# A retention block's group norm: v's rows freed of their mean ahead of the split, the variance from ScalarE's squares, the gate product as a plain instruction

## The chip, the cores and the metric

The kernel runs on one core of a Trainium2 chip. The core has TensorE (PE, matrix products into eight banks of PSUM), VectorE (DVE), ScalarE (ACT), GpSimd (POOL, which also issues DMAs) and SyncE (SP, which issues DMAs). Each engine works through its own queue in order and waits for others by semaphores. The metric is device time in microseconds (us), less is better. The kernel before takes 1023.57 us, the median of three runs from 1023.52 to 1023.67.

## The reference

One layer of a bidirectional encoder on x of 512 tokens by 1024 features, in float32: a combined projection of the normed x, a gated short convolution, a bidirectional retention with four heads, a merge of both with two gates, a SwiGLU feed-forward part and a last norm. What the change touches is the retention's end. With P[n, m] the decayed scores of a head (512 by 512, both directions together) and v its values (512 tokens by 512 features):

```
ret = P @ v                                   # per head, 512 x 512
mu  = mean(ret, over the 512 features)
var = mean((ret - mu)^2, over the 512 features)
ret = (ret - mu) * rsqrt(var + EPS) * g_ret
y_r = (ret * silu(g_sw)) @ w_r_out
```

The mean of a row of ret is the same sum over m, with P's weights, of the means of v's rows. If every row of v has mean zero, mu is zero for every row of ret, and var is the mean of its squares.

## The kernel before

Every float32 product is done as three products of a high and a low part (`mm3`, lines 340 to 344): a factor is rounded into its high part by ScalarE and the rest is taken by VectorE, in `split` (lines 200 to 210). Weights come by DMA into raw tiles, are split the same way (lines 203 and 204) and used from five buffers.

The work runs in this order: projections (to about 378 us), the retention heads (378 to 602 us), the output projections with a Strassen scheme, the feed-forward part, the last norm. q, k, v and the swish gate sg of each head were written to DRAM earlier and are loaded again one head ahead by `load_head` (lines 858 to 861), at the top of the iteration before.

The loop of the heads (lines 948 to 967) does, for head h:

- `do_pv(p, vv, sg)` (lines 884 to 905): for each of four blocks of 128 rows, twelve products into one bank (128 x 512), ret of these rows. VectorE reads the bank for the statistics (`bn_stats`, line 894; `bn_aggr`, 895), adds EPS (896); POOL raises to the power of -1/2 (897); VectorE forms (ret - mu) times the gate from the bank (903), which sets the bank free; ScalarE scales the result by the power (905). Behind the last block's power POOL issues four DMAs that add up weights for W_o in DRAM (`sum_step`, lines 265 to 274, of which 272 adds and 274 copies).
- `do_scores` for head h + 1 (lines 863 to 876): four banks of 24 products in all, times the decay table on VectorE (873), split into p.
- `split_v` for head h + 1 (lines 878 to 882): two calls of `split` on halves of 128 x 1024.
- `do_t` for head h (lines 907 to 913): sixteen transposes on VectorE (line 218), then four scaled splits (206 on ScalarE, 207 on VectorE) into yr.
- the convolution's last part (`do_mix(3)`, for h = 0), or `do_wr(h - 1)` (lines 927 to 940): the product of the head before with its rows of W_r, two halves of four banks with 48 products each; the banks are emptied by ScalarE (935, for head 0) or VectorE (937).

The convolution's `z_forms` (lines 789 to 806) of `do_mix` runs beside the first blocks of `do_pv` of heads 0 and 1; it uses up to ten scratch tiles of 128 x 512 (`t512`, nine buffers) that are free again when POOL's DMAs (line 633) have stored them.

Nothing in this code fixes the order on an engine but the `issue_after` blocks. A scheduler orders the instructions of each engine when the program is built: by its model of the times, among those that are ready the one that comes first in the program. Buffers of a pool are handed out in that order too. So an edit at one place can shift the order elsewhere.

Of the kernel before, what the change touches and what calls it, by code (L numbers as in the profile page):

```python
# [12 lines left out]
F32 = mybir.dt.float32  # L13
F32R = mybir.dt.float32r
AF = mybir.ActivationFunctionType
ALU = mybir.AluOpType

P = 128
# [3 lines left out]
NB = S // P  # L22
HEADS = 4
QK = 256
VD = 512
FF = 2816
NFB = FF // P
EPS = 1e-6
# [143 lines left out]
def block_kernel(ctx: ExitStack, tc: tile.TileContext, xw0, xw, xT, xtok, wpack, wquad, cols, decs, rot, g_ffn, g_final, out):  # L172
    nc = tc.nc
# [5 lines left out]
    small = ctx.enter_context(tc.tile_pool(name="small", bufs=4))  # L179
# [8 lines left out]
    def bigtile(dt=F32, n=4):  # L188
        return big.tile([P, n, 512], dt, tag="big", name="big", padded_shape=[P, 4, 512])

    def t512(dt=F32):
        return tmp.tile([P, 512], dt, tag="t512", name="t512")

    def bank():
        return psum.tile([P, 512], F32, tag="bank", name="bank")
# [4 lines left out]
    def split(src, hi, lo, scale=None, round=None):  # L200

        if scale is None:
            first = (round or nc.scalar.copy)(hi, src)  # L203
            low_of[0] = nc.vector.tensor_tensor(out=lo, in0=src, in1=hi.bitcast(F32), op=ALU.subtract)  # L204
        else:
            first = nc.scalar.activation(hi, src, AF.Copy, scale=scale)
            nc.vector.scalar_tensor_tensor(
                out=lo, in0=src, scalar=scale, in1=hi.bitcast(F32),
                op0=ALU.mult, op1=ALU.subtract)
        return first  # L210
# [54 lines left out]
    def sum_step(behind, among="quads"):  # L265

        if steps[among]:
            quad, f, g, u, add = steps[among].pop(0)
            src = wsum[quad, g, u] if g[0] == "t" else quarter(quad, g, u)
            with tc.issue_after(behind.ins):  # L270
                if add:
                    nc.gpsimd.dma_start(out=wsum[quad, f, u], in_=src, accum_op=ALU.add, max_dma_last_dim=4 * CH)
                else:
                    nc.gpsimd.dma_start(wsum[quad, f, u], src)
# [65 lines left out]
    def mm3(ps, left, right, first, last):  # L340
        (lh, ll), (rh, rl) = left, right
        nc.tensor.matmul(ps, lh, rh, start=first, stop=False)  # L342
        nc.tensor.matmul(ps, lh, rl, start=False, stop=False)  # L343
        nc.tensor.matmul(ps, ll, rh, start=False, stop=last)  # L344
# [293 lines left out]
    for h in range(EARLY):  # L638
        pss = [bank() for _ in range(4)]
        for kk in range(8):  # L640
# [4 lines left out]
            if (h, kk) == (1, 1):  # L645
# [3 lines left out]
                for k in range(8):  # L649
                    xk = x_in(k)  # L650
                    nc.vector.scalar_tensor_tensor(out=xs[k // 4][:, k % 4, :], in0=xk, scalar=gmix[:, k:k + 1], in1=rrow,
                                                   op0=ALU.mult, op1=ALU.mult)
# [13 lines left out]
        t = bigtile()  # L666
# [21 lines left out]
    for n, i, o in (("a11", 0, 0), ("a12", 1, 0), ("a22", 1, 256)):  # L688
# [16 lines left out]
                            op0=ALU.mult, op1=ALU.add)  # L705
    for j in range(15, 0, -2):
# [3 lines left out]
                                   op0=ALU.mult, op1=ALU.mult)  # L710
# [166 lines left out]

    def split_v(v):
        vv = (bigtile(F32R), bigtile(F32R))
        for k in (0, 2):  # L880
            split(v[:, k:k + 2, :], vv[0][:, k:k + 2, :], vv[1][:, k:k + 2, :])
        return vv

    def do_pv(p, vv, sg):

        for nb in range(NB):
            ps = bank()
            sl = slice(nb * P, (nb + 1) * P)
            for mb in range(NB):
                mm3(ps, (p[0][:, mb, sl], p[1][:, mb, sl]), (vv[0][:, mb, :], vv[1][:, mb, :]),  # L890
                    mb == 0, mb == NB - 1)
            st = small.tile([P, 6], F32, tag="bnst", name="bnst")
            mv = small.tile([P, 4], F32, tag="bnmv", name="bnmv")
            nc.vector.bn_stats(st, ps)
            nc.vector.bn_aggr(mv[:, 0:2], st)
            nc.vector.tensor_scalar_add(mv[:, 2:3], mv[:, 1:2], EPS)
            power = nc.gpsimd.tensor_tensor(out=mv[:, 3:4], in0=mv[:, 2:3], in1=mhalf[:, 0:1], op=ALU.pow)
            if nb == NB - 1:

                for _ in range(4):  # L900
                    sum_step(power, "heads")
            t = sg[:, nb, :]
            nc.vector.scalar_tensor_tensor(out=t, in0=ps, scalar=mv[:, 0:1], in1=t,
                                           op0=ALU.subtract, op1=ALU.mult)
            nc.scalar.activation(t, t, AF.Copy, scale=mv[:, 3:4])

    def do_t(h, t):
# [35 lines left out]
    nxt = load_head(0)  # L943
    p = do_scores(nxt[0], nxt[1])
    vv, sg = split_v(nxt[2]), nxt[3]
    do_mix(2)
    yr = None
    for h in range(HEADS):
        if h < HEADS - 1:
            nxt = load_head(h + 1)  # L950
        else:
            load_z((0,))
        do_pv(p, vv, sg)
        t = sg
        if h < HEADS - 1:
            p = do_scores(nxt[0], nxt[1])
            vv, sg = split_v(nxt[2]), nxt[3]
        else:
            load_z((1, 2))
        new = do_t(h, t)  # L960
        if h == 0:
            do_mix(3)
        else:
            if h == HEADS - 1:
                sgr = [load(t) for t in grd]
            do_wr(h - 1, yr)
        yr = new
# [456 lines left out]
```

## Time and profile before

| | before |
|---|---|
| timed runs, median (lowest to highest) | 1023.57 us (1023.52 to 1023.67) |
| profiled execution: span, first to last instruction | 1021.7 us |
| TensorE clock granted, mean | 0.999 |
| busy: PE, weight load, DVE | 1013.2, 883.2, 902.5 us |
| busy: ACT, POOL | 548.4, 151.7 us |
| instructions | 14821 |
| DMA | 202.34 MB, mean 198 GB/s |

The profile is of one execution. Its own time is given as the span; the timed runs are measured from outside of it. Busy time counts an engine's instructions, not the waits and the issuing of DMAs. PEld is the load of weights into the array, which overlaps the products. In a row of grouped instructions stand line, engine, operation, output and inputs with partitions x elements, the count, then busy time in us and the mean of one in ns, then idle time of the engine just ahead of them and what ended it. In a timeline a row has its start and its length in us; several like instructions in a row are merged, with their count. A wait has the waiting instruction, what it waited for, the sum in us, how often, and the longest.

### The profile page before, as it was taken

Reading aid. Unit: us, or ns where it says so; the run is one execution under the profiler, and the core shown is the slowest. Engines: PE = TensorE matmul, PEld = TensorE weight load, DVE = VectorE, ACT = ScalarE, POOL = GpSimd, SP = SyncE. Lnnn points to the kernel's source line nnn. Section 1 sums busy time; section 2 is a strip of 40 time slices with the busy share of each in tenths; the row PEclk is TensorE's granted clock in tenths of the full one; section 3 lists DMA queues with packets and bytes.
Section 4 is the critical chain, followed back from the end, with each engine's and each line's share of the span. In section 5 each row is a group of like instructions: output and inputs, shape, how many; then the busy total and the mean of one; then the engine's idle time right before and its main releaser. Section 6 shows DMA issues by size and latency. Waiting matters only on the chain.

```text
span 1021.7 us, 14821 instructions
## 1 busy us (share of the span) xinstructions
PE 1013.2 (99%) x5586; PEld 883.2 (86%) x5586; DVE 902.5 (88%) x1161; ACT 548.4 (54%) x744; POOL 151.7 (15%) x238
## 2 busy tenths in 40 slices
PE   9999999999999999999999999999999999999997
PEld 7888888888888998888888888889998999899986
DVE  7878998979798888797989997999898999889996
ACT  7547665553655455343543325586654565556554
POOL 0030221222122003202122100020001410110011
PEclk9999999999999999999999999999999999999999
DMA  9525587695767657839597855484316562663523
GB/s 354 188 81 185 173 296 212 214 310 162 249 196 238 250 203 268 333 130 349 124 331 294 272 200 169 157 264 132 107 42 242 172 154 83 198 153 104 165 69 98
DMA packets 53992, 202.34 MB, mean 198 GB/s; under 512 B 7392, under 2 KB 7520, under 8 KB 49312
## 3 DMA queue, kind: packets, MB, share of 16 engines
q1 hardware_dynamic: 37600, 137.39, 39.0%
q0 software_dynamic: 16032, 63.71, 21.3%
q8 instruction: 44, 0.72, 0.3%
q10 hardware_dynamic: 288, 0.29, 0.1%
q14 instruction: 28, 0.23, 0.1%
HBM read 162.82 MB, written 57.41 MB: 216 GB/s over the span
## 4 chain that ended last, share of the span: by engine, by line
PE 98%; DVE 1%; ACT 0%; issue 0%; POOL 0%; POOLq 0%; ACTq 0%
PE bank L427 39%; PE bank L383 27%; PE bank L342 10%; PE bank L343 10%; PE bank L344 10%; PE bank L477 0%; PE bank L1053 0%; PE bank L998 0%; PE bank L662 0%; DVE raw L301 0%; DVE big L1296 0%; ACT whi L203 0%; DVE wlo L204 0%; POOL fin L1286 0%; POOL ac L1035 0%
## 5 line engine op out<-in xcount | busy, mean ns | idle before, releaser
L203 ACT CAST whi<-raw 128x1024 fp32r<-128x1024 f32 (+2 forms) x299 | 302.8, 1028 | 265.0 <-PE bank L427 67.1
L204 DVE TENSOR_TENSOR wlo<-raw,whi 128x1024 fp32r<-128x1024 f32 (+2 forms) x300 | 352.7, 1192 | 68.0 <-ACT whi L203 67.7
L383 PE MATMUL bank<-xform,whi 128*128 128x256 f32 x1424 | 258.2, 284 | 0.3 <-ACT whi L203 0.3
L383 PEld LDWEIGHTS bank<-xform,whi 128*128 128x128 f32 x1424 | 222.3, 192 | 2.0 <-ACT t L434 0.8
L383 PE MATMUL bank<-xform,wlo 128*128 128x256 f32 x712 | 200.7, 283 | 0.0
L427 PE MATMUL bank<-whi,big 128*128 128x512 f32 x596 | 187.0, 389 | 0.0
L427 PE MATMUL bank<-whi,xform 128*128 128x512 f32 x496 | 157.1, 390 | 0.0
L301 DVE TENSOR_TENSOR raw<-raw 128x1024 f32<-128x1024 f32 (+1 forms) x128 | 152.0, 1203 | 4.2 <-DMA raw<-wquad 3.3
L383 PEld LDWEIGHTS bank<-xform,wlo 128*128 128x128 f32 x712 | 136.4, 192 | 0.0
L427 PEld LDWEIGHTS bank<-whi,big 128*128 128x128 f32 x596 | 111.9, 188 | 23.8 <-ACT t L434 0.4
L427 PE MATMUL bank<-wlo,big 128*128 128x512 f32 x298 | 115.7, 389 | 0.0
L427 PEld LDWEIGHTS bank<-whi,xform 128*128 128x128 f32 x496 | 93.0, 188 | 19.7 <-DVE xform L204 0.6
L427 PE MATMUL bank<-wlo,xform 128*128 128x512 f32 x248 | 96.5, 389 | 0.0
L434 ACT COPY t<-bank 128x512 f32<-128x512 f32 x105 | 61.0, 587 | 56.3 <-PE bank L383 30.1
L342 PE MATMUL bank<-big,whi 128*128 128x512 f32 x220 | 85.7, 390 | 0.0
L344 PE MATMUL bank<-big,wlo 128*128 128x512 f32 x220 | 85.6, 389 | 0.0
L343 PE MATMUL bank<-big,whi 128*128 128x512 f32 x220 | 85.6, 389 | 0.0
L427 PEld LDWEIGHTS bank<-wlo,big 128*128 128x128 f32 x298 | 56.0, 188 | 11.4
L427 PEld LDWEIGHTS bank<-wlo,xform 128*128 128x128 f32 x248 | 46.6, 188 | 9.6
L342 PE MATMUL bank<-whi,big 128*128 128x512 f32 x128 | 49.8, 389 | 0.0
L343 PE MATMUL bank<-wlo,big 128*128 128x512 f32 x128 | 49.8, 389 | 0.0
L344 PE MATMUL bank<-whi,big 128*128 128x512 f32 x128 | 49.8, 389 | 0.0
(203 smaller groups left out, 1385.8 us busy)
## 6 DMA issues: line engine op xcount, KB each, us to landing
raw<-wquad SPq DMA_DIRECT2D x140, 512.0 KB, 4.7
raw<-wpack SPq DMA_DIRECT2D x42, 512.0 KB, 6.3
t_f<-wquad POOLq DMA_DIRECT2D x12, 512.0 KB, 8.0
z<-t POOLq DMA_DIRECT2D x24, 256.0 KB, 4.5
t_o<-wquad POOLq DMA_DIRECT2D x12, 512.0 KB, 6.7
zform<-z POOLq DMA_DIRECT2D x6, 1024.0 KB, 7.8
v<-t POOLq DMA_DIRECT2D x16, 256.0 KB, 5.7
sg<-t POOLq DMA_DIRECT2D x16, 256.0 KB, 4.8
```

The lines of the kernel that those rows point to most:

```text
L203: first = (round or nc.scalar.copy)(hi, src)
L204: low_of[0] = nc.vector.tensor_tensor(out=lo, in0=src, in1=hi.bitcast(F32), op=ALU.subtract)
L301: nc.vector.tensor_tensor(out=t, in0=t, in1=raws[quad, more, u][:, 0:n], op=ALU.add)
L342: nc.tensor.matmul(ps, lh, rh, start=first, stop=False)
L343: nc.tensor.matmul(ps, lh, rl, start=False, stop=False)
L344: nc.tensor.matmul(ps, ll, rh, start=False, stop=last)
L383: nc.tensor.matmul(o, l[:, c], r[:, k], start=start and s == 0 and k == 0 and i == 0, stop=stop and k == 3 and i == 2, skip_group_check=True)
L427: nc.tensor.matmul(pss[tt], l, r[:, c], start=start and k == 0 and i == 0, stop=stop and k == n - 1 and i == 2, skip_group_check=True)
L434: nc.scalar.copy(t, ps)
```

## The change

In `split_v` each row of v (a token, on its partition) gets the mean of its 512 features taken away ahead of the split. ScalarE copies each of four 128 x 512 parts onto itself with a running sum; POOL multiplies the four sums by -1/512; ScalarE writes the high part as a copy of v plus that number, and VectorE the low part as v plus the number less the high part. Two casts and two subtractions of 128 x 1024 become four sums, one small product, four shifted copies and four subtractions with a scalar operand of 128 x 512.

In `do_pv` the two instructions of the statistics go. ScalarE squares the bank, scaled by 1/sqrt(512), into a scratch tile that nobody reads, with a running sum, which is the variance. The addition of EPS moves from VectorE to POOL. The gate product no longer takes the mean away and is a product of two operands. A bank is now free when both ScalarE's squares and the gate product have read it.

```
@@ split_v
         vv = (bigtile(F32R), bigtile(F32R))
-        for k in (0, 2):
-            split(v[:, k:k + 2, :], vv[0][:, k:k + 2, :], vv[1][:, k:k + 2, :])
+        m = small.tile([P, 8], F32, tag="mean", name="mean")
+        for k in range(NB):
+            nc.scalar.activation(v[:, k, :], v[:, k, :], AF.Copy, accum_out=m[:, k:k + 1])
+        nc.gpsimd.tensor_scalar_mul(m[:, 4:8], m[:, 0:4], -1.0 / VD)
+        for k in range(NB):
+            off = m[:, 4 + k:5 + k]
+            nc.scalar.activation(vv[0][:, k, :], v[:, k, :], AF.Identity, bias=off)
+            nc.vector.scalar_tensor_tensor(out=vv[1][:, k, :], in0=v[:, k, :], scalar=off,
+                                           in1=vv[0][:, k, :].bitcast(F32), op0=ALU.add, op1=ALU.subtract)
         return vv
@@ do_pv
-            st = small.tile([P, 6], F32, tag="bnst", name="bnst")
             mv = small.tile([P, 4], F32, tag="bnmv", name="bnmv")
-            nc.vector.bn_stats(st, ps)
-            nc.vector.bn_aggr(mv[:, 0:2], st)
-            nc.vector.tensor_scalar_add(mv[:, 2:3], mv[:, 1:2], EPS)
+            nc.scalar.activation(t512(), ps, AF.Square, scale=VD ** -0.5, accum_out=mv[:, 1:2])
+            nc.gpsimd.tensor_scalar_add(mv[:, 2:3], mv[:, 1:2], EPS)
             power = nc.gpsimd.tensor_tensor(out=mv[:, 3:4], in0=mv[:, 2:3], in1=mhalf[:, 0:1], op=ALU.pow)
...
-            nc.vector.scalar_tensor_tensor(out=t, in0=ps, scalar=mv[:, 0:1], in1=t,
-                                           op0=ALU.subtract, op1=ALU.mult)
+            nc.vector.tensor_tensor(out=t, in0=ps, in1=t, op=ALU.mult)
             nc.scalar.activation(t, t, AF.Copy, scale=mv[:, 3:4])
```

## The prediction

> **What bounds the kernel now.** I read the page first (busy shares, chain), then the waits of TensorE (PE), then the busy time by stretches, then the timelines around the retention heads, where all edits lie.
>
> ```profile
> span 1021.7 us, 14821 instructions
> ...
> PE 1013.2 (99%) x5586; PEld 883.2 (86%) x5586; DVE 902.5 (88%) x1161; ACT 548.4 (54%) x744; POOL 151.7 (15%) x238
> ...
> PE 98%; DVE 1%; ACT 0%; issue 0%; POOL 0%; POOLq 0%; ACTq 0%
> ```
> ```profile
> PE bank L477 <- DVE t L474: 1.4, 1, 1.4
> PE bank L1053 <- DVE t L1039: 0.5, 1, 0.5
> PE bank L383 <- ACT whi L203: 0.3, 1, 0.3
> ```
> ```profile
> 378.50:602.30 223.80, 223.80 (x1011) 186.06 (x1010) 198.85 (x306) 86.16 (x119) 45.93 (x74) 1.00 0.75 258
> 602.30:690.00 87.70, 87.07 (x427) 72.82 (x427) 79.63 (x98) 56.07 (x81) 6.30 (x12) 1.00 0.61 198
> 690.00:800.00 110.00, 109.66 (x791) 103.19 (x790) 100.62 (x122) 65.58 (x90) 4.46 (x8) 1.00 0.43 139
> ...
> 1004.00:1021.70 17.70, 11.61 (x52) 9.28 (x50) 10.67 (x20) 7.69 (x20) 4.11 (x8) 0.96 0.32 119
> ```
> The first fence: PE is busy 1013.2 of 1021.7 us, and 98% of the chain that ended last is PE. The second is the whole list of what PE ever waited for: 1.4 us at the start, 0.5 and 0.3 us far behind the heads. The third (columns: stretch, length, then busy time of PE, weight load, VectorE (DVE), ScalarE (ACT), GpSimd (POOL), then clock, DMA) puts the heads into 378.5 to 602.3: PE is busy for every one of the 223.8 us, at clock 1.00. VectorE has 199 us of work in it, ScalarE 86. So the change works on engines that are nowhere last in their stage. What is idle on PE and could come back behind the heads is 0.63 us (87.70 less 87.07) and 0.34 us (110.00 less 109.66); the 6.1 us at the end are the tail of the last norm, which the change doesn't touch. No gain can be over 0.97 us unless PE itself gets less work, and it gets none: the edits leave every matmul.
>
> The span, 1021.7, is what the sum is made against. The timed runs have a median of 1023.57, which is 1.87 more; that lies outside the first and last instruction, and I carry it unchanged.
>
> **The change part by part.** The rows of the terms, from the grouped lines (count, busy us, mean ns of one, idle before):
>
> ```profile
> L937 DVE TENSOR_TENSOR big<-bank,big 128x512 f32<-128x512 f32 x24 | 15.3, 682 | 0.1
> L903 DVE SCALAR_TENSOR_TENSOR big<-bank,bnmv,big 128x512 f32<-128x512 f32 x16 | 11.9, 742 | 0.0
> L894 DVE BATCH_NORM_STATS2 bnst<-bank 128x6 f32<-128x512 f32 x16 | 11.1, 692 | 1.5 <-PE bank L344 1.5
> ...
> L204 DVE TENSOR_TENSOR big<-big 128x1024 fp32r<-128x1024 f32 x8 | 9.7, 1217 | 0.0
> ...
> L779 DVE SCALAR_TENSOR_TENSOR big<-u,cols_sb,big 128x512 f32<-128x512 f32 x8 | 6.0, 750 | 0.9 <-ACT big L777 0.8
> ...
> L895 DVE BATCH_NORM_AGGREGATE bnmv<-bnst 128x2 f32<-128x6 f32 x16 | 2.9, 180 | 1.1
> ...
> L896 DVE TENSOR_SCALAR bnmv<-bnmv 128x1 f32<-128x1 f32 x16 | 2.5, 153 | 0.5
> ```
> ```profile
> L905 ACT ACTIVATE big<-big,bnmv 128x512 f32<-128x512 f32 x16 | 11.4, 722 | 28.6 <-POOL bnmv L897 27.4 <-DVE big L903 1.3
> ...
> L203 ACT CAST big<-t 128x512 fp32r<-128x512 f32 x16 | 9.7, 616 | 5.9 <-DVE t L873 5.9
> L203 ACT CAST big<-big 128x1024 fp32r<-128x1024 f32 x8 | 8.4, 1049 | 0.0
> ...
> L935 ACT COPY big<-bank 128x512 f32<-128x512 f32 x8 | 4.1, 603 | 0.0
> ```
> ```profile
> L1031 ACT ACTIVATE t<-big 128x512 f32<-128x512 f32 x8 | 5.0, 629 | 0.0
> ...
> L749 ACT ACT_TABLE_LOAD x2 | 2.6, 1283 | 0.0
> ...
> L1031 ACT ACTIVATION_READ_ACCUMULATOR t<-big 128x1 f32 x8 | 1.5, 189 | 0.0
> ```
> ```profile
> L897 POOL TENSOR_TENSOR bnmv<-bnmv,mhalf 128x1 f32<-128x1 f32 x16 | 9.0, 589 | 43.8 <-DVE bnmv L896 43.8
> ...
> L1033 POOL TENSOR_SCALAR ac<-ac 128x1 f32<-128x1 f32 x4 | 1.2, 308 | 76.8 <-ACT t L1031 76.8
> ```
> VectorE: the statistics go, 16 x (692 + 180 + 153) = 16.4 us less. The gate product loses its scalar operand: 16 x (742 - 682, L937 being a plain product-like instruction from PSUM) = 1.0 less. In the split of v, eight subtractions of 1024 become sixteen of 512 with a scalar: 16 x 750 (L779 is that shape) - 9.7 = 2.3 more. Net 15.1 us less.
>
> ScalarE: 16 running sums over v and 16 squares with a sum, each 629 + 189 = 818 ns: 26.2 us more. Sixteen shifted copies in place of eight casts: 16 x 722 - 8.4 = 3.2 more. (The shifted copy isn't in the trace. Its ends: 603 as L935's plain copy, and 722 as L905, which like it reads an operand per row; I take 722. At worst it needs a table load, 1283 ns as L749, and one back for each head.) Net 29.4 us more, 86 to 116 of 224.
>
> GpSimd: 16 additions of EPS and 4 scalings, 308 ns as L1033: 6.2 us more, of 46 to 52 in 224.
>
> All of this lies beside PE's 223.8 us, so at these prices the sum on the path is nothing: 0. What hides it is that each product has its inputs long before PE comes to it, and the question is where this cover is thinnest. The link within one row block doesn't get longer: statistics to scaling now takes 1.93 us where DVE starts on time (estimate from the parts: 692 + 180 + 153 + 589 and hops, 1.6 to 2), and the new one is 629 + 189 + 308 + 589 = 1.72 and hops. That chain only sets when the gated block is complete, and behind it stand the transposes on VectorE. There the cover is thin at one place, head 1's transposes:
>
> ```profile
> 479.85 0.42 DVE L204 TENSOR_TENSOR t<-big,t 128x256 fp32r<-128x256 f32 x1 [2.05 <-DMA z<-t]
> ...
> 493.45 11.45 DVE L218 STREAM_TRANSPOSE big<-big 32x512 f32<-32x512 f32 x16
> ```
> ```profile
> 507.41 2.02 ACT L935 COPY big<-bank 128x512 f32<-128x512 f32 x4
> ```
> ```profile
> 509.63 0.39 PE L342 MATMUL bank<-big 128*128 128x512 f32 x1
> ```
> The transposes run from 493.45 to 504.9; ScalarE's scaled splits of the transposed head follow, and queued behind those are the evictions of do_wr's first four banks (L935). Head 2's first product (PE at 509.63) needs the first of these banks: all eight are taken by then (four of do_wr's first half, four of its second). The first eviction ends at 507.41 + 0.60 = 508.0, so the cover is 1.6 us. If the transposes start after 495.05, PE stands.
>
> Will they? The new work in front of them is split_v's for head 2: sums on ScalarE, the scaling on POOL, shifted copies on ScalarE, then the new subtractions on VectorE, which wait for these and have the transposes queued behind them. VectorE's load in that stretch:
>
> ```profile
> 471.50:482.40 10.90, 10.90 (x49) 9.03 (x49) 8.25 (x18) 3.58 (x6) 6.12 (x10) 1.00 0.97 383
> 482.40:487.90 5.50, 5.50 (x26) 4.53 (x25) 5.06 (x12) 3.31 (x6) 3.12 (x7) 1.00 0.46 164
> 487.90:509.60 21.70, 21.70 (x97) 17.99 (x96) 21.46 (x30) 9.97 (x16) 1.59 (x2) 1.00 0.62 145
> ```
> VectorE has 34.8 of 38.1 us there and loses, for one head, 15.1 / 4 = 3.8; ScalarE has 16.9 and gains 29.4 / 4 = 7.4. The best case: scores end on PE at 487.9, their last split is done 2.0 later (a VectorE pass, 0.68 as L937, the cast, 0.62 as L203, a second pass), transposes start at about 490, 3.5 us earlier than now and worth nothing to PE. The worst is the first rival. I take a start within 1 us of 493.45: VectorE's relief and ScalarE's longer queue about cancel (ScalarE from 472.5: the convolution's four last casts 2.3 at 0.6 each, four squares 3.3, four scalings 2.9, four sums 3.3, four shifted copies 2.9, four score casts 2.5, together 17.2 us, to 489.7 without waits; with 0.9 us of waiting per row block to 493.3, and a last subtraction of 0.75). So no stall: 1021.7 of span, 1023.5 us.
>
> **The rivals.** *First: ScalarE works in series at head 1 (slower).* Its queue is in order, and each scaling waits for the power on POOL. The squares write a scratch tile from the same nine as the convolution's store tiles, for one of which VectorE waited until 479.85. If the first square starts only then and each block runs as 1.72 + 0.2 of hops + 0.72 = 2.6 us, the fourth ends at 490.4; then, if nothing was filled in between, sums 3.3, score casts 2.5, POOL 0.3, shifted copies 2.9, last subtraction 0.75: 500.2. The transposes start 6.7 us late, less 1.6 of cover: PE loses 5.1, time 1028.7. Half of the sums filled in between takes away half of the excess: 1026. Against it: v of head 2 is loaded ahead of its head, so its sums need no result of this head and can fill ScalarE's gaps, since the order on an engine is by readiness. It decides above 1.6 us of delay. With table loads (2 x 1.28) alone, the loss would be 1.0: 1024.6, within the bound below.
>
> *Second: POOL is late for the scaling of v's mean (slower).* POOL also issues the DMAs that add up weights for W_o, and at head 2 it stands there for a landing:
>
> ```profile
> 530.24 0.80 POOL L272 DMA_DIRECT2D t_o<-wquad x1 [0.70 <-DMA t_o<-t_o]
> ```
> ```profile
> 530.07 11.44 DVE L218 STREAM_TRANSPOSE big<-big 32x512 f32<-32x512 f32 x16
> 541.55 1.29 DVE L937 TENSOR_TENSOR big<-bank,big 128x512 f32<-128x512 f32 x2
> ```
> ```profile
> 547.71 0.39 PE L342 MATMUL bank<-big 128*128 128x512 f32 x1
> ```
> ```profile
> 805.94 7.34 POOL L1247 TENSOR_SCALAR mark<-t 128x1 f32<-128x1 f32 x1 [17.56 <-DVE t L1139]
> ```
> ```profile
> 805.76 1.22 DVE L204 TENSOR_TENSOR wlo<-raw,whi 128x1024 fp32r<-128x1024 f32 x1
> ...
> 813.20 0.69 DVE L1192 TENSOR_TENSOR t<-bank,t 128x512 f32<-128x512 f32 x1
> ```
> If the scaling for head 3 stands behind that issue it runs at 531.0; shifted copies 2.9, subtraction 0.75, transposes at 535.0 instead of 530.07, 4.9 late. The cover is 542.2 (first eviction by L937) to 547.71, 5.5 us: still enough. But the last fence shows a 128x1 instruction on POOL that took 7.34 us where its like took 0.31: it ended at 813.28, when VectorE went from a run of subtractions on SBUF to one that reads PSUM (813.20). VectorE's splits come in twos of 1.22 here, so such a delay adds about 2.4, and PE loses 1.8 at head 2 and, on top of the middle course, 0.8 to 1.8 at head 1: 3, time 1026.5. [...] Against the rival: after the change VectorE's blocks are mostly products from PSUM at that place, which end such a run.
>
> *Third: VectorE's relief reaches the idle PE behind the heads.* It would return 0.97: 1022.6. Against it: the 0.5 us wait at L1053 is for a chain of ScalarE, POOL and VectorE 85 us behind the heads.
>
> **How the numbers follow.** A measurement can tell about 0.2% from no change, 2.05 us. Forecast (nothing moves on PE, give or take 0.5): 0.70. Third rival: 0.04, also within the bound. First rival: 0.15, of which 0.12 over the bound; second 0.06, half of it over. A reordering elsewhere, since the order of all engines is worked out anew: 0.05, of which 0.03 costs PE more than the bound and 0.02 saves as much. Faster 0.02, slower 0.12 + 0.03 + 0.03 = 0.18, same 0.80. The range runs from the third rival (1022.6) to the first one's middle course (1026) and leaves out about 0.14: the first rival's upper half, a part of the second, the reorderings.
>
> **What would show it.** Right: PE busy 1013.2 with no new row among its waits; VectorE about 887 busy, ScalarE about 578; L894 to L896 gone; head 1's transposes starting before 495. Wrong: a wait of PE for ScalarE's L935 or VectorE's L937, about 510 or 548, of over 2 us, with the late shifted copies ahead of it; POOL's scaling at several us instead of 0.3; table loads between the shifted copies and the squares.

## The result, and the profile after

The changed kernel takes 1031.12 us (median of four runs, 1028.31 to 1031.4), the kernel before beside it 1023.55 (four runs, 1022.47 to 1023.67): a ratio of 1.0067, 95% interval 1.0052 to 1.0082. It is slower by 0.7%, and it lies outside the predicted range. A second set of five runs gave 1029.17 (1026.76 to 1030.23) against 1023.32, ratio 1.0054 (1.0041 to 1.0067).

The profiled execution spans 1029.6 us against 1021.7, 7.9 more. Its page and the list of what PE waited for:

```profile
span 1029.6 us, 14855 instructions
...
PE 1016.4 (99%) x5586; PEld 885.3 (86%) x5586; DVE 888.5 (86%) x1121; ACT 569.7 (55%) x816; POOL 159.8 (16%) x258
```
```profile
PE bank L342 <- ACT big L939: 2.3, 1, 2.3
PE bank L383 <- ACT whi L203: 1.9, 1, 1.9
PE bank L477 <- DVE t L474: 1.4, 1, 1.4
PE bank L342 <- DVE big L908: 0.8, 1, 0.8
PE bank L1057 <- DVE t L1043: 0.5, 1, 0.5
```
VectorE's busy time fell by 14.0 us and ScalarE's rose by 21.3, and the time went up all the same. The new rows among the waits say where: PE waits 2.3 us for the eviction that was line 935 (now 939), 0.8 us for the gate product (908), and 1.9 instead of 0.3 us in the feed-forward part. PE itself is busy 3.2 us longer with the same 5586 products. Together 2.3 + 0.8 + 1.6 + 3.2 = 7.9: the whole difference.

The 3.2 us are a matter of the clock. The busy times of three stretches (columns as in the prediction; PE's clock is the third number from the end), and PE's timeline around the first wait:

```profile
510.72:514.13 3.41, 1.51 (x7) 1.25 (x8) 3.41 (x6) 3.41 (x8) 0.00 (x0) 1.00 0.45 154
514.13:517.54 3.41, 3.41 (x10) 2.63 (x9) 1.64 (x2) 3.41 (x6) 0.00 (x0) 0.50 0.47 124
...
794.02:797.44 3.42, 3.42 (x16) 3.42 (x17) 3.42 (x4) 1.77 (x2) 0.49 (x1) 0.50 0.49 164
```
```profile
490.32 0.50 PE L342 MATMUL bank<-whi,big 128*128 128x512 f32 x1 [0.82 <-DVE big L908]
...
512.62 0.50 PE L342 MATMUL bank<-big 128*128 128x512 f32 x1 [2.28 <-ACT big L939]
...
513.19 0.40 PE L344 MATMUL bank<-big 128*128 128x512 f32 x1
513.42 0.40 PE L342 MATMUL bank<-big 128*128 128x512 f32 x1
...
514.51 0.63 PE L343 MATMUL bank<-big 128*128 128x512 f32 x1
514.94 0.63 PE L344 MATMUL bank<-big 128*128 128x512 f32 x1
...
517.75 0.39 PE L342 MATMUL bank<-big 128*128 128x512 f32 x1
```
Between 514.1 and 517.5 the clock is 0.50 and the products start every 0.43 us instead of every 0.23: eight of them at 0.2 more, 1.6 us. The same happens once behind the 1.9 us wait (clock 0.50 from 794.02 to 797.44), 1.6 again. So 4.7 of the 7.9 us belong to head 1 (2.3, 0.8 and 1.6), and 3.2 to the feed-forward part.

Why head 1 is late is in the timelines of ScalarE and VectorE, of the stretch for which the prediction counted the queue:

```profile
471.95 0.62 ACT L203 CAST t<-big 128x512 fp32r<-128x512 f32 x1
479.62 0.64 ACT L882 ACTIVATE big<-big 128x512 f32<-128x512 f32 x1 [7.05 <-DMA big<-v]
...
480.25 0.60 ACT L203 CAST t<-t 128x512 fp32r<-128x512 f32 x1
...
483.44 0.58 ACT L900 ACTIVATE t<-bank 128x512 f32<-128x512 f32 x1
...
486.76 2.21 ACT L909 ACTIVATE big<-big,bnmv 128x512 f32<-128x512 f32 x3 [1.51 <-POOL bnmv L902]
488.87 0.58 ACT L900 ACTIVATE t<-bank 128x512 f32<-128x512 f32 x1
...
490.53 0.72 ACT L909 ACTIVATE big<-big,bnmv 128x512 f32<-128x512 f32 x1 [0.99 <-POOL bnmv L902]
...
512.00 2.02 ACT L939 COPY big<-bank 128x512 f32<-128x512 f32 x4
```
```profile
480.88 0.69 DVE L204 TENSOR_TENSOR t<-t,t 128x512 fp32r<-128x512 f32 x1 [5.51 <-ACT t L203]
...
489.57 0.69 DVE L908 TENSOR_TENSOR big<-bank,big 128x512 f32<-128x512 f32 x1 [3.55 <-ACT t L900]
...
498.06 11.44 DVE L218 STREAM_TRANSPOSE big<-big 32x512 f32<-32x512 f32 x16
```
ScalarE's queue has the first sum over v of head 2 (L882) ahead of three of the convolution's casts (L203). That sum waits for the load of v, issued at 469.97 and there at 479.6, and ScalarE stands for 7.05 us with work behind it that was ready. VectorE waits 5.51 us for a cast, the convolution's stores come late, and so do the squares (L900) behind the sums. The fourth square is queued behind three scalings (L909), which wait for POOL's powers; the fourth gate product starts when that square is done, and PE, which needs this bank, waits 0.8. The transposes start at 498.06 instead of 493.45, the evictions at 512.00 instead of 507.41.

The load of v is itself late. Before, it was issued at 468.80 and took 7.1 us, so it landed at 475.9; now it takes 9.6. The view of that one load, before:

```profile
L855 SPq DMA_DIRECT2D big<-v x1: 326/326/326, 468.8 to 468.8; - x1
...
DMA to landing us min/median/max: 7.1/7.1/7.1
```
This begins at head 0: its transposes start at 445.71 instead of 443.03, VectorE's work behind them (L779) is late by as much, and SyncE's queue stands for that work shortly ahead of the load. With the old landing, ScalarE, whose last cast ahead of the sum ends at 472.6, would have stood for about 3.3 us instead of 7.05 (an estimate from these times).

### The profile page after: what moved, and what is told of

It is laid out like the page before. It is cut to its first block, busy times and chain, and to the rows that moved or that the text cites. A ratio compares the mean times of both kernels' runs of the same rounds, so it can differ in the third digit from the quotient of the medians.

```text
span 1029.6 us, 14855 instructions
## 1 busy us (share of the span) xinstructions
PE 1016.4 (99%) x5586; PEld 885.3 (86%) x5586; DVE 888.5 (86%) x1121; ACT 569.7 (55%) x816; POOL 159.8 (16%) x258
## 4 chain that ended last, share of the span: by engine, by line
PE 73%; issue 16%; DVE 4%; POOL 3%; DMA 2%; ACT 1%; POOLq 0%; ACTq 0%; DVEq 0%
PE bank L427 33%; PE bank L383 21%; PE bank L342 6%; PE bank L343 6%; PE bank L344 6%; POOL z L633 1%; DMA z<-t 1%; DVE big L218 1%; DMA raw<-wquad 1%; DVE wlo L204 1%; POOL bnmv L902 0%; PE bank L477 0%; ACT whi L203 0%; PE bank L1057 0%; DVE raw L301 0%
## 5 line engine op out<-in xcount | busy, mean ns | idle before, releaser
L203 ACT CAST whi<-raw 128x1024 fp32r<-128x1024 f32 (+2 forms) x299 | 302.7, 1028 | 242.7 <-PE bank L427 64.8
```

## The experiments

The theory: the order on ScalarE's queue, not the work that was added, makes head 1 late; PE loses what exceeds a cover of 1.6 us. Against it stood that one half of the change is too dear by itself, or that added ScalarE time costs wherever it is put. The first four kernels shared one chip (before, there: 1023.55), the other four a second one (before: 1023.32).

**The edits of `do_pv` alone.** `split_v` stays as before.

```
-            nc.vector.bn_stats(st, ps)
-            nc.vector.bn_aggr(mv[:, 0:2], st)
-            nc.vector.tensor_scalar_add(mv[:, 2:3], mv[:, 1:2], EPS)
+            nc.scalar.activation(t512(), ps, AF.Square, scale=VD ** -0.5, accum_out=mv[:, 1:2])
+            nc.gpsimd.tensor_scalar_add(mv[:, 2:3], mv[:, 1:2], EPS)
...
+            nc.vector.tensor_tensor(out=t, in0=ps, in1=t, op=ALU.mult)
```


> Only the edits in do_pv (squares with a running sum, EPS on POOL, plain gate product); the split of v is as before, so v keeps its mean: the kernel leaves the subtraction of the mean out. Theory (ScalarE's queue stands at the sums over v for the landing of v's load, with the convolution's casts behind them): there are no such sums, head 1's transposes start at 493 to 494.5 as before, PE waits for no eviction there, 1023 to 1024 us. Rival A (the series of square, POOL and scaling per row block makes the chain late by itself): transposes at 495.5 or later, PE loses 1 to 3 us at the first eviction of do_wr, 1025 to 1029 us.

Measured: 1024.05 us (1023.48 to 1025.94, eleven runs), ratio 1.0006 (0.9997 to 1.0015). ScalarE's timeline has a wait of its own:

```profile
481.23 0.60 ACT L893 ACTIVATE t<-bank 128x512 f32<-128x512 f32 x1 [4.45 <-DMA z<-t]
```
The square waits for a scratch tile that the convolution's store still holds, as the first rival had supposed. But the transposes start at 493.83, 0.4 late, and PE waits only for what it waited for before. This half stays within the cover, as the theory had it.

**The edits of `split_v` alone.** `do_pv` stays as before.

```
-        for k in (0, 2):
-            split(v[:, k:k + 2, :], vv[0][:, k:k + 2, :], vv[1][:, k:k + 2, :])
+        for k in range(NB):
+            nc.scalar.activation(v[:, k, :], v[:, k, :], AF.Copy, accum_out=m[:, k:k + 1])
...
```


> Only the edit in split_v (sums, POOL's scaling, shifted copies); do_pv as before. Theory: the sums over head 2's v stand ahead of two or three of the convolution's casts on ScalarE until the load lands (about 479.6), these casts come some 4 us late as in the changed kernel, the transposes start at 496.5 to 498.5, PE loses 1.5 to 3.5 us before head 2's first product, 1025 to 1028 us and 1.6 more in executions in which the clock then falls. Rival A (the series in do_pv is the cause): PE loses under 0.5, 1023 to 1024 us.

Measured: 1025.17 us (1024.35 to 1027.22, eleven runs), ratio 1.0018 (1.0009 to 1.0026). ScalarE's timeline, then VectorE's transposes:

```profile
478.45 0.63 ACT L882 ACTIVATE big<-big 128x512 f32<-128x512 f32 x1 [5.38 <-DMA big<-v]
```
```profile
494.70 11.45 DVE L218 STREAM_TRANSPOSE big<-big 32x512 f32<-32x512 f32 x16
```
ScalarE stands for the load here too. The transposes are 1.25 late, still ahead of the 495.05 from which PE should stand, and PE doesn't wait at head 1. The theory had expected 496.5 to 498.5 and a wait of 1.5 to 3.5 us: this it got wrong, the sums ahead of the casts aren't enough by themselves. The time is within its range by another route: what this profile has over the one before, 1.3 us of span, is mostly a longer wait in the feed-forward part (1.2 instead of 0.3). So neither half makes the loss at head 1; the two together are 4.6 late, much more than 0.4 + 1.25. The late casts delay the convolution's stores and the squares, and only where the squares too are in ScalarE's queue does that reach the gated blocks: the fourth gate product starts at 486.34 here, 0.9 late, and at 489.57 in the changed kernel, 4.1 late.

**The whole change, with the sums over v held behind the convolution's last cast.**

```
-            split(t, *hl)
+            casts.append(split(t, *hl))
...
+        with tc.issue_after(casts[-1].ins):
+            for k in range(NB):
+                nc.scalar.activation(v[:, k, :], v[:, k, :], AF.Copy, accum_out=m[:, k:k + 1])
```


> The whole change, with the sums over v held behind the convolution's last cast on ScalarE. Theory: the casts come at 474 to 477 again, POOL's stores and the scratch tiles are free some 4 us earlier than in the changed kernel, the transposes start at 494 to 496, PE loses 0 to 1 us there, 1023.5 to 1025 us. Rival B (the added work in front of the transposes is what counts, wherever the sums stand): transposes at 497.5 to 498.5 as in the changed kernel, PE loses 2 to 3, 1027 to 1031 us.

Measured: 1025.02 us (1023.84 to 1025.81, eleven runs), ratio 1.0012 (1.0003 to 1.0021). PE's waits, then ScalarE's timeline:

```profile
...
PE bank L342 <- ACT big L942: 1.4, 1, 1.4
PE bank L383 <- ACT whi L203: 0.7, 1, 0.7
```
```profile
474.90 0.62 ACT L203 CAST t<-t 128x512 fp32r<-128x512 f32 x1 [2.04 <-DVE t L805]
...
478.92 0.63 ACT L885 ACTIVATE big<-big 128x512 f32<-128x512 f32 x1 [2.31 <-DMA big<-v]
...
482.51 0.60 ACT L903 ACTIVATE t<-bank 128x512 f32<-128x512 f32 x1 [2.29 <-DMA z<-t]
```
One edit of the order takes back most of the loss: the casts are early again. (Not all of the gain is head 1's: the feed-forward wait is 0.7 here instead of 1.9, and no slow stretch follows it.) What is left is the first sum's wait for v (2.31) and the second square's for a scratch tile (2.29), with the other sums queued behind it. The transposes start at 496.31, 1.26 behind 495.05, and PE waits 1.4, a little more than the theory had expected (496 at the latest, up to 1 us) and far from the rival's 497.5. The clock stays up (1.00 from 510 to 518 us).

**v centred where it is made.** The sum, a small scaling and a shifted copy, all on ScalarE, sixteen times in the projections; `split_v` as before, `do_pv` changed.

```
+    def centre(t):
+        m = small.tile([P, 2], F32, tag="mean", name="mean")
+        nc.scalar.activation(t, t, AF.Copy, accum_out=m[:, 0:1])
+        nc.scalar.activation(m[:, 1:2], m[:, 0:1], AF.Copy, scale=-1.0 / VD)
+        nc.scalar.activation(t, t, AF.Identity, bias=m[:, 1:2])
```


> v freed of its mean where it is made (in the projections, ahead of its store: sum, small scaling and shifted copy on ScalarE for each 128 x 512 block, 16 in all), split_v as before, do_pv as in the change. Theory: no sum waits for a load in the heads, and the projections' stage has ScalarE at 57%: no new wait of PE, 1023 to 1024 us, at best up to 1 us under the kernel before. Rival C (added ScalarE work of about 28 us costs wherever it is put): 1025 us or more, with PE waiting for ScalarE in the projections.

Measured: 1025.62 us (1024.68 to 1026.29, eleven runs), ratio 1.0021 (1.0011 to 1.0030). PE's waits have a row of the projections instead:

```profile
PE bank L427 <- DVE wlo L204: 0.8, 1, 0.8
```
There is no wait of PE at head 1, but the work is not free in the projections either: 0.8 us of this wait, and PE busy 1014.7 instead of 1013.2. Laid product by product beside the kernel before, PE is 1.0 late at this wait, 0.1 at each of five other places between 100 and 215 us, where v is made, and 0.3 in the first 8 us; what causes the small ones wasn't followed up. The time is the one that the rival gave (1025 or more): added ScalarE work costs here, though it need not, as the whole change in another order shows below.

**The changed kernel again**, on the second chip.

> The changed kernel a second time, for a second trace and more times. Theory: the wait at the first eviction of do_wr (2.3 us at head 2's first product) comes again, within 0.5 us, since it follows from the orders on the engines and the landing of v's load; whether the clock then falls for one stretch of 3.4 us, 1.6 us of time, differs from execution to execution, so the times lie in two groups about 1028 and 1031. Rival D (the loss is something that came once in that execution): the wait is under 1 us.

Measured: the 1029.17 us above; span of the profiled execution 1028.5.

```profile
PE bank L342 <- ACT big L939: 2.3, 1, 2.3
PE bank L342 <- DVE big L908: 1.7, 1, 1.7
PE bank L383 <- ACT whi L203: 1.5, 1, 1.5
```
The waits at head 1 are there again, that for the gate product longer. PE is busy 1014.8, 1.6 more than before: one stretch of low clock, behind the 2.3, and none behind the 1.5. So the wait at head 1 is the kernel's. The two groups of times that were expected, about 1028 and 1031, didn't show: the five lie between 1026.76 and 1030.23. As far as two profiles tell, the run time moves with the clock, the feed-forward wait and the wait for the gate product.

**The whole change in another order.** Beside the held sums, the squares write a scratch tile of their own, and the four scalings of a head are held behind its fourth square.

```
...
+            sq = nc.scalar.activation(junk, ps, AF.Square, scale=VD ** -0.5, accum_out=mv[:, 1:2])
...
+            scaled.append((t, mv))
+        with tc.issue_after(sq.ins):
+            for t, mv in scaled:
+                nc.scalar.activation(t, t, AF.Copy, scale=mv[:, 3:4])
```


> The whole change, with the order on ScalarE put right in three places: the sums over v behind the convolution's last cast, the squares written to a scratch tile of their own, the four scalings of a head behind its fourth square. Theory (the loss is order on one queue, not work): head 1's transposes start at 492 to 494, PE waits for no eviction there, 1023 to 1024 us. Rival B (the added work in front of the transposes costs by itself): transposes at 496 or later, 1025 us or more.

Measured: 1023.17 us (1022.3 to 1024.26, eleven runs), ratio 0.9999 (0.9990 to 1.0007): no difference from before. Its page's busy times, PE's whole list of waits, and the evictions at head 1:

```profile
PE 1013.2 (99%) x5586; PEld 883.4 (86%) x5586; DVE 888.5 (87%) x1121; ACT 569.0 (56%) x816; POOL 159.7 (16%) x258
```
```profile
PE bank L477 <- DVE t L474: 1.4, 1, 1.4
PE bank L1066 <- DVE t L1052: 0.5, 1, 0.5
```
```profile
506.53 2.02 ACT L948 COPY big<-bank 128x512 f32<-128x512 f32 x4
```
All the added and removed work is in it (VectorE 888.5, ScalarE 569.0, as in the changed kernel), and the loss is gone. So it was the order, with the scratch tiles that the squares share with the convolution, and not the work. How much each of the three edits gives isn't separated. They also act through head 0, whose transposes start at 443.62 (445.57 with the sums alone held): v's load lands at 476.0 here instead of 478.9, and the sums no longer wait for it. The run also answers the third rival: 14 us off VectorE are worth nothing to PE.

**The kernel before, its evictions at head 1 put off.** Two idle copies on ScalarE stand ahead of the first evictions; the scheduler put a weight cast between them.

```
...
+                        with tc.issue_after(yr_last[0].ins):
+                            for _ in range(2):
+                                late[:] = [nc.scalar.copy(delay, delay)]
+                    with tc.issue_after(late[0].ins):
+                        nc.scalar.copy(t, ps)
```


> The kernel before, with two idle copies (128 x 512, on a tile of zeros that nobody else uses) and the weight cast that follows put ahead of the evictions of do_wr's first half for head 0 on ScalarE: some 2.2 us of delay. With a cover of 1.6 us there, PE loses 0.3 to 1 us before head 2's first product, the clock stays: 1023.9 to 1024.6 us. If the cover isn't this one (another wait ends last): no new wait, 1023.5.

Measured: 1024.28 us (1023.24 to 1026.55, eleven runs), ratio 1.0012 (1.0003 to 1.0021). ScalarE, then PE's wait:

```profile
509.39 3.97 ACT L942 COPY big<-bank 128x512 f32<-128x512 f32 x8
```
```profile
PE bank L342 <- ACT big L942: 0.3, 1, 0.3
```
The evictions start 2.0 us late, and PE waits 0.3: a cover of 1.7.

**The same with five idle copies.**

```
-                            for _ in range(2):
+                            for _ in range(5):
```


> The same with five idle copies, some 4.1 us of delay: PE loses 2.1 to 3 us, 1025.6 to 1026.6, and 1.6 us more in executions in which the clock then falls to a half for 3.4 us (1027.2 to 1028.2). If a wait of that size doesn't touch the clock: never over 1026.8.

Measured: 1026.92 us (1025.17 to 1028.39, five runs), ratio 1.0035 (1.0023 to 1.0048). ScalarE, PE's wait, and a stretch behind it:

```profile
511.95 4.00 ACT L942 COPY big<-bank 128x512 f32<-128x512 f32 x8
```
```profile
PE bank L342 <- ACT big L942: 2.7, 1, 2.7
```
```profile
510.00:515.00 5.00, 2.42 (x6) 1.93 (x7) 1.69 (x2) 4.91 (x11) 0.00 (x0) 0.73 0.58 186
```
Evictions 4.5 late, PE waits 2.7: a cover of 1.8. PE's clock falls as in the changed kernel (0.73 here), and PE is busy 1.9 us longer than before. A late eviction alone, with none of the change, gives two of the three parts of the loss at head 1, the wait for the eviction and the slow stretch behind it; the wait for the gate product it doesn't give.

## Why the prediction was wrong

The place was right, and so was the point from which it decides. Each kernel's start of head 1's transposes against the predicted 495.05 (left out are v centred where it is made, which reaches the heads later, and the two kernels with idle copies, which put off the evictions alone):

| kernel | transposes start | ahead of or behind 495.05 | PE's wait for the eviction |
|---|---|---|---|
| whole change, other order | 492.58 | 2.47 ahead | none |
| before | 493.45 | 1.60 ahead | none |
| `do_pv` alone | 493.83 | 1.22 ahead | none |
| `split_v` alone | 494.70 | 0.35 ahead | none |
| sums behind the casts | 496.31 | 1.26 behind | 1.4 |
| the change | 498.06 | 3.01 behind, 2.19 less PE's own 0.82 | 2.3 |
| the change again | 498.90 | 3.85 behind, 2.19 less PE's own 1.66 | 2.3 |

**The step that failed** is "I take a start within 1 us of 493.45". It rested on a count of ScalarE's queue (17.2 us of work from 472.5) with 0.9 us of waiting for each row block, and on the argument against the first rival: "v of head 2 is loaded ahead of its head, so its sums need no result of this head and can fill ScalarE's gaps". They need no result, but they need the load, which lands at 479.6, seven microseconds into that count (before, at 475.9, it was 3.4; the count has no term for either). Being free of the head put the sums early in the queue, ahead of the casts, and there ScalarE stood for 7.05 us. The argument that was to make the first rival unlikely is the mechanism that brought it about. The sign that was named for being wrong came with it: a wait of PE of over 2 us for that eviction, behind late shifted copies.

**The first rival** came true in its place and its sign, by another route. It had the squares wait for the convolution's store tiles and each block run in series, transposes 6.7 late and 5.1 us lost. The store tiles do hold the squares up where the casts are early (4.45 in `do_pv` alone, 2.29 with the sums held), but in the changed kernel the load of v comes first: 4.6 late, 3.1 us of waits at head 1. Its chance had been put at 0.15.

**A term was missing.** No case counted what a wait of PE does to the clock: 3.2 of the 7.9 us. By the waits alone the changed kernel would have spanned 1026.4. One of its four timed runs did about that (span 1026.5, mean clock 0.999, against 0.995 in the profiled one); another spanned 1029.2 at a mean clock of 0.998, so the clock is not all that differs between runs.

**The feed-forward wait** (1.9 instead of 0.3) isn't explained. The order of the instructions on each engine is the same there in both kernels; VectorE waits there for a load of weights:

```profile
786.71 2.36 DVE L301 TENSOR_TENSOR raw<-raw 128x1024 f32<-128x1024 f32 x2 [2.02 <-DMA raw<-wquad]
```
Before, it waited 0.76 for it at 780.58. Between the profiled executions PE's wait there goes from none (`do_pv` alone, the other order) through 0.3 (before, five idle copies) to 1.9, with no clear line to the work of the change: the other order has all of that work, and five idle copies reach that place 4.6 us late and wait no longer for it. The load is not issued late, it takes longer: 5.2 us from issue to landing where PE doesn't wait, 5.4 where it waits 0.3, 6.3 where it waits 1.2 and 1.5, 6.6 in the changed kernel. What makes it slow stays open, and with it whether the change has a part in these 3.2 us (1.6 of wait, 1.6 of clock).

**The prices** of single instructions were near enough. VectorE lost 14.0 us (15.1 predicted), ScalarE gained 21.3 (29.4). From the changed kernel's grouped lines:

```profile
L886 ACT ACTIVATE big<-big,mean 128x512 fp32r<-128x512 f32 x16 | 11.0, 718 | 0.0
...
L900 ACT ACTIVATE t<-bank 128x512 f32<-128x512 f32 x16 | 9.4, 592 | 8.2 <-PE bank L344 5.1 <-DMA z<-t 3.1
...
L882 ACT ACTIVATION_READ_ACCUMULATOR big<-big 128x1 f32 x16 | 3.0, 187 | 0.0
L883 POOL TENSOR_SCALAR mean<-mean 128x4 f32<-128x4 f32 x4 | 1.0, 248 | 57.8 <-ACT big L882 57.7
```
The shifted copy took 718 ns (722 taken), with no table load beside it; the square 592 and its read-out about 190 (629 and 189 taken). What the sum had wrong for ScalarE is the overlap: the measured parts add up to 28.7 us, but an instruction starts some 0.1 us ahead of its predecessor's end (the cast at 471.95 behind one that began at 471.00 and took 1.05), and with 72 more instructions that is some 7 us less of busy time.

**The second rival** did not come about: POOL's scaling took 248 ns, and at head 2 it ran ahead of the DMA for which POOL stands there. **The third** was worth nothing, as the other order shows.

## What to carry to other kernels

Work that depends on nothing but a load is not free filling: in a queue that runs in order it can be put ahead of work that is ready, and then the engine stands for the load with all of that behind it (ScalarE here for 7.05 us). Look where such work is queued, what lies behind it, and when its load lands. Where one engine is busy 99% of the time, a count of busy time on the others decides little (14.0 us less on VectorE and 20.6 more on ScalarE, in the other order, gave 1023.17 us against 1023.32); find the eviction with the least time to spare, and follow each queue up to it by its waits, not by its sums.

## What the runs showed of the hardware

A short wait of PE can cost 1.6 us beyond its own length. Behind waits of 2.3 and 1.9 us (the change), 2.3 (the change again) and 2.7 us (five idle copies) the products started every 0.43 instead of 0.23 us, or with 256 columns every 0.21 instead of 0.12, until some 3 us later (the clock was 0.50 in both stretches of the change); behind waits of 1.4 (sums held), 1.5 and 1.7 us (the change again) they did not.

What goes with it shows in where the slow stretches lie. The two of the changed kernel are 3.41 us long each and start at 514.13 and 794.02, 279.9 us apart, which is 82 times 3.413. The profiles of the kernel before and of the changed one also have one at their end, in the last norm, from 1020.39 and 1026.13; counted back from the latter in steps of 3.413 us, the two others of the changed kernel start on a step too (150 and 68 steps). The 3.41 us just ahead of a stretch held 1.90 and 1.93 us without a product (the change), 2.28 (the change again) and 2.47 (five idle copies); ahead of the two in the last norm it was 3.42 (the kernel before) and 2.60 (the change). No other step of these two profiles between the first 8 us and the last norm, counted back from the last stretch of each, held more than 0.74. One in the last norm of the kernel before, from 1013.56, held 1.36, and the clock behind it was 1.00. The wait of 1.7 us in the change again, by steps counted back from its slow stretch, is cut by the end of one into 0.94 and 0.72. So in these runs it is the idle time within one step that goes with a slow stretch, not the length of the wait: 1.36 us did not bring one, 1.90 did. Whether a wait of 2 us that falls across the end of a step costs 1.6 more was not shown.

On POOL a 128x1 addition took 2.06 us instead of 0.22 while VectorE ran subtractions on SBUF until 560.86 (POOL's timeline of the changed kernel, then VectorE's). It cost nothing here:

```profile
558.87 2.06 POOL L901 TENSOR_SCALAR bnmv<-bnmv 128x1 f32<-128x1 f32 x1 [2.48 <-ACT t L900]
```
```profile
558.51 2.35 DVE L204 TENSOR_TENSOR wlo<-raw,whi 128x1024 fp32r<-128x1024 f32 x2
```
